# Two stages of a hybrid block stack read their 256-token operands from addresses 64 bytes off a multiple of 128

## The chip, the cores and the metric

One NeuronCore of a Trainium2 chip runs the whole program in a single launch. The metric is the device time of one execution in microseconds. The kernel before takes 2101.51 us, the median of three runs (2100.49 to 2103.12). One execution was profiled; all rows below come from it.

## The reference, cut to what matters

The program computes two layers of a hybrid block (chunk attention, a depthwise convolution and a retention mixer, then a squared-ReLU MLP) and one layer of a second block (differential attention beside a state-space layer, then a gated feed-forward with a 3-tap convolution) on 512 tokens of width 1024, all in float32. The two stages that the change is about are these:

```python
# first block, second of two layers, after the mixers
x = x + rms_norm(mix, g_mix_post)
h = rms_norm(x, g_mlp_pre)                                  # (512, 1024)
f = jnp.square(jax.nn.relu(h @ w_up)) @ w_down              # w_up 1024 x 4096, w_down 4096 x 1024
# second block
hn = rmsnorm(h, norm2_gain[i])
up = causal_dwconv(hn @ w_up[i], conv_w[i], conv_b[i])      # w_up 1024 x 5632
gate, val = jnp.split(up, 2, axis=-1)
h = h + (jax.nn.silu(gate) * val) @ w_down[i]               # w_down 2816 x 1024
```

## The kernel before, in words

**Precision.** Every float32 operand is split in two float32r parts, a rounded one (names ending in `hi`) and the rest (`lo`), and a product is three matmuls: weights hi by input hi, weights hi by input lo, weights lo by input hi (`mm3`). A matmul holds a 128 x 128 operand in the array and streams a moving operand of N columns, one column per token or per output feature. A row such as `ps<-hhi,whi` reads: into PSUM tile `ps`, moving operand `hhi`, held operand `whi`.

**The transposed input.** After each norm, `to_hT` transposes the normed tokens and writes them to `hhi` and `hlo`, two tiles of 128 partitions x 8 x 512 (features by tokens) that live for the whole program. The projections of the mixers use them as moving operand with all 512 tokens, as held operand (for outputs that keep tokens on the partitions, the weights then stream in 384 or 512 columns), and at a stage's start by halves of 256 tokens.

**The two fast stages.** The MLP of the second hybrid layer and the feed-forward of the second block compute `h @ w_up` by a Strassen-like scheme with seven products in place of eight (`FastUp`): a unit makes two output tiles of 128 features x 512 tokens from seven products of 256 tokens each, four of them with halves of `hhi` and `hlo`, three with sums of blocks. `fast_in` makes the sums once a stage: `shi` and `slo`, twelve tiles of 128 x 512. The first four output tiles of each stage are computed plainly, in halves of 256 tokens (`f_split`). So every up-projection matmul of these stages streams 256 columns. The down-projections between them stream weights in 512 columns, with `fhi` and `flo` held.

**What sets the order.** The Python code does not issue instructions; `Trace` records them with a due time. `order` then plans: it walks through time with its own costs, gives a free engine the ready instruction that is due first, chooses between ScalarE, VectorE and GpSimd where an instruction may run on more than one of them, and gives each tile a slot of its pool at its first instruction. An instruction whose tile finds no free slot, or whose slot an earlier one is promised, is passed over (`room`). The planned list is issued as it stands (line 674 is the one line that issues, so all rows of the profile carry it); each engine runs its own part of the list in order.

**Where tiles lie.** Pools are laid out one after the other. Tiles of the pool without slots (`cp`) lie where they are first placed; `mhalf`, `hhi` and `hlo` are placed first. Behind them come the weight pools and `sp`, 58 general slots of 2048 bytes per partition for nearly every other tile (`s2` takes from it), then small ones. `hhi` starts at byte 2304 of a partition, `hlo` at 18688, the slots of `sp` from 104192 on: all multiples of 128. Slices of them start at multiples of 512 bytes. So each float32r moving operand of the program starts at a multiple of 128 bytes.

Of the kernel before, what the change touches and what calls it, by code (L numbers as in the profile page):

```python
# [11 lines left out]
F32R = mybir.dt.float32r  # L12
# [5 lines left out]
P = 128  # L18
S = 512
# [917 lines left out]
class Builder:  # L937
# [11 lines left out]
    def __init__(self, tc, ctx, A, out):  # L949
        self.tc, self.nc, self.A, self.out = tc, Trace(tc.nc), A, out  # L950

        def pool(name, bufs, shape=None, dtype=F32, space="SB"):
            kw = {} if space == "SB" else {"space": bass.MemoryType.PSUM if space == "PS" else bass.MemoryType.DRAM}
            return Pool(lambda n: ctx.enter_context(tc.tile_pool(name=n, bufs=1, **kw)), name, bufs, shape, dtype, space)
        self.cp = pool("cp", None)
        self.wr = pool("wr", self.NR, [P, 1024])
        self.wh, self.wl = pool("wh", self.NW, [P, 1024], F32R), pool("wl", self.NW, [P, 1024], F32R)
        self.sp = pool("sp", 86 - 2 * self.NR - 4 * self.NW, [P, 512])
        self.stp = pool("stp", 16, [P, 32])
        self.jp = pool("jp", 2, [P, 512], BF16)  # L960
        self.psp = pool("psp", 4, [P, 512], F32, "PS")
        self.pss = pool("pss", 4, [P, 512], F32, "PS")
        self.dp = pool("dp", None, space="DRAM")
        self.side = Side(self)
        self.T = 30000.0
        self.in_side = False
        self.wbias = 2
        self.rawT = None
        self.before = None
        self.seven = False  # L970
# [164 lines left out]
    def fast_in(self):  # L1135

        nc, R = self.nc, self.rawT
        self.rawT = None
        S = {}
        for j in range(2):  # L1140
            s1, s2, s4, s3 = (self.s2(name="sraw") for _ in range(4))
            nc.sub(s1, R[1, j], R[1, j + 2], self.wbias)
            nc.sub(s2, s1, R[0, j], self.wbias)
            nc.sum(s4, R[0, j + 2], s2, self.wbias)
            nc.sub(s3, R[0, j], R[1, j], self.wbias)
            for i, s in ((6, s2), (5, s1), (3, s4)):
                hi, lo = self.s2(F32R, "shi"), self.s2(F32R, "slo")
                nc.copy(hi, s)
                nc.sub(lo, s, hi.bitcast(F32), self.wbias)
                S[i, j] = [z.rearrange("p (k n) -> p k n", k=2) for z in (hi, lo)]  # L1150
            hi, lo = (z[:, 2 * j:2 * j + 2, 256:512] for z in (self.hhi, self.hlo))
            v = s3.rearrange("p (k n) -> p k n", k=2)
            nc.copy(hi, v)
            nc.sub(lo, v, hi.bitcast(F32), self.wbias)

        def a(i, k):
            if i == 1:
                return self.hT(k, 0, 256)
            if i == 2:
                return self.hT(k + 4, 0, 256)  # L1160
            if i == 4:
                return self.hT(k + 4, 256, 512)
            if i == 7:
                return self.hT(k, 256, 512)
            return tuple(z[:, k % 2, :] for z in S[i, k // 2])
        return a
# [11 lines left out]
    def fast_end(self, steps=(4, 3)):  # L1178
        if self.before:
            for i in steps:  # L1180
                self.before.run(i)
            if 3 in steps:
                self.before = None

    def run(self):
        nc, tc, A = self.nc, self.tc, self.A
        self.pvt = self.cp.tile(F32, "pv", [P, PV_N])
        self.cm = self.cp.tile(F32, "cm", [P, 4 * P])
        self.rope = self.cp.tile(F32, "rope", [P, NT, 64])
        self.hhi = self.cp.tile(F32R, "hhi", [P, KD, S])  # L1190
        self.hlo = self.cp.tile(F32R, "hlo", [P, KD, S])
        self.mhalf = self.cp.tile(F32, "mhalf", [P, 32])
        self.ident = self.cm[:, 0:P]
        self.blk64 = self.cp.tile(F32R, "blk64", [P, P])
        self.blk16 = self.cm[:, 2 * P:3 * P]
        self.tri = self.cm[:, 3 * P:4 * P]
        self.ones = self.cp.tile(F32R, "ones", [P, P])
        self.epsc = self.cp.tile(F32, "epsc", [P, 1])
        self.ws = Stream(self, A["wst"], stream_spec())
        X = [[self.s2(name="X") for _ in range(2)] for _ in range(NT)]  # L1200
        gpre = [self.s2(name="gain") for _ in range(2)]

        def load_x(t):
            for h in range(2):
                nc.sync.dma_start(out=X[t][h], in_=A["x"][t * P:(t + 1) * P, 512 * h:512 * (h + 1)])
        nc.vector.memset(self.mhalf, -0.5)
        nc.vector.memset(self.ones.bitcast(F32), 1.0)
        nc.vector.memset(self.epsc, EPS)
        self.prio(-8000.0)
        load_x(0)  # L1210
        for h in range(2):
            nc.sync.dma_start(out=gpre[h], in_=A["gains"][0, :, 512 * h:512 * (h + 1)])
        nc.sync.dma_start(out=self.ident, in_=A["cmat"][:, 0:P])
        self.prio(0.0)
        load_x(1)
        hs = {}
        for t in range(2):
            hs[t] = self.pre_norm(t, X, gpre)
            self.to_hT(t, hs.pop(t))
        self.prio(4000.0)  # L1220
        self.wbias = 3
        self.ws.prep_to(2)
        self.prio(8000.0)
        for t in (2, 3):
            load_x(t)
            hs[t] = self.pre_norm(t, X, gpre)
        self.prio(20000.0)
        nc.sync.dma_start(out=self.pvt, in_=A["pvec"])
        nc.sync.dma_start(out=self.cm[:, P:], in_=A["cmat"][:, P:])
        nc.vector.tensor_copy(self.blk64, self.cm[:, P:2 * P])  # L1230
        nc.sync.dma_start(out=self.rope, in_=A["rope2"].rearrange("t p n -> p t n"))
        del X
        self.pending = hs
        self.xd = None
        self.prio(self.T)
        for l in range(LAYERS):
            self.hybrid(l)
        self.second()
# [294 lines left out]
    def hybrid(self, l):  # L1533
# [8 lines left out]
            return tt  # L1542
        tabs = []
        for t in range(NT):
            z = self.s2(name="rtab")
            nc.sync.dma_start(out=z[:, :RT_N], in_=A["rtab"][t])
            tabs.append(z)

# [24 lines left out]

        def rot(w):
            def f(t, ps):
                d = self.s2(name="rqk")
                self.ret_rot(t, ps, w, tabs[t], d)
                qk[w].append(d)
            return f
# [39 lines left out]
        self.t_unit(lambda t, ps: p0.__setitem__(t, ps), 512, mix, 4, W_OUT_KS, need)  # L1619
        self.side.drain()  # L1620
        self.rawT = {} if l in FAST else None
        self.finish(lambda t: (p0[t],), 4, W_OUT_KS, mix, X, gpost, gpre)
        self.mix = {}
        (self.mlp if l in FAST else self.mlp_plain)(l, X)
# [152 lines left out]

    def finish_mlp(self, f, acc, xm, gpost, gpre, store):
        nc = self.nc
        ks = sorted(f)  # L1780
        lhs = lambda k, t0, t1: tuple(z[:, t0:t1] for z in f[k])
        nch = len(ks) // 2
        ws = [self.ws.take() for _ in range(2 * nch)]
        hs, X = {}, {}
        for t in range(NT):
            X[t] = [self.s2(name="X") for _ in range(2)]
            for h in range(2):
                nc.sync.dma_start(out=X[t][h], in_=xm[t][h])
                ps = self.ps()
                for c in range(nch):  # L1790
                    self.t_part(ps, ws[h * nch + c], ks[2 * c:2 * c + 2], t, 512, lhs, c == 0, c == nch - 1)
                nc.vector.tensor_tensor(acc[t][h], ps, acc[t][h], op=ALU.add)
            self.post_update(t, acc[t], X, gpost)
            if 1 <= t <= 2:
                self.to_hT(t - 1, hs.pop(t - 1))
            hs[t] = self.pre_norm(t, X, gpre)
            store(t, X)
            X.pop(t)
        self.pending = hs
# [246 lines left out]
    def dq_evac(self, p, t, ps, cg, sg):  # L2046
# [5 lines left out]
        nc.vector.tensor_scalar(st[:, 0:8], st[:, 0:8], EPS, None, op0=ALU.add)  # L2052
        nc.gpsimd.tensor_tensor(st[:, 8:16], st[:, 0:8], self.mhalf[:, :8], op=ALU.pow)
        nc.vector.tensor_scalar(self.rq[:, p, :, t], st[:, 8:12], 0.125, None, op0=ALU.mult)
        a, b, d = self.s2(), self.s2(), self.s2(name="dqk")
        v4 = lambda z: z.rearrange("p (a g d) -> p a g d", a=2, d=64)
        tb = lambda z: z.rearrange("p (a d) -> p a d", a=2).unsqueeze(2).to_broadcast([P, 2, 4, 64])
        nc.vector.tensor_tensor(v4(a), v4(ps), tb(cg[:, t * P:(t + 1) * P]), op=ALU.mult)
# [71 lines left out]
    def second(self):  # L2130
# [11 lines left out]
        self.nlam = st[:, 5:6]  # L2142
        nc.vector.tensor_scalar(st[:, 6:7], self.pvt[:, PV["subln"][0]:PV["subln"][0] + 1], 1.0 - LAM_INIT, None, op0=ALU.mult)
        self.subl = st[:, 6:7]
        self.mask = self.s2(name="mask")
        nc.gpsimd.memset(self.mask[:, :384], 0.0)
        nc.gpsimd.tensor_copy(self.mask[:, 384:], self.tri)
        self.rq = self.cp.tile(F32, "rq", [P, 4, 4, NT])
        cg, sg = self.s2(name="cg"), self.s2(name="sg")
        go = PV["gqk"][0]  # L2150
        gv = self.pvt[:, go:go + 128].rearrange("p (a d) -> p a d", d=32)
        for t in range(NT):
# [116 lines left out]
        ws = [self.ws.take() for _ in range(4)]  # L2269
        hs = {}  # L2270
        self.rawT = {}
        for t in range(NT):
            ps = self.ps()
            for c in range(4):
# [54 lines left out]
@with_exitstack  # L2329
def hybrid_stack_kernel(ctx: ExitStack, tc, A, out):  # L2330
    b = Builder(tc, ctx, A, out)
    b.run()
    order = b.nc.order()
    for t in (b.mhalf, b.hhi, b.hlo):
        t.place()
    with tc.manual_schedule():
        b.nc.issue(order)
# [18 lines left out]
```

## Time and profile before

| | |
|---|---|
| runs | 2100.49, 2101.51, 2103.12 us; median 2101.51 |
| the profiled execution | 2105.0 us, its span from the first to the last instruction 2103.3 us |
| TensorE (PE) | busy 2015.8 us, 96% of the span, 11188 matmuls; mean granted clock 0.988 of 2.4 GHz |
| weight loads (PEld) | 1745.7 us, beside the matmuls |
| VectorE (DVE) | 1527.6 us, 73% |
| ScalarE (ACT) | 1042.0 us, 50% |
| GpSimd (POOL) | 691.8 us, 33% |
| fast stage of the first block | up to 1215 us; its matmuls of 256 columns begin at about 890 us |
| fast stage of the second block | from about 1740 us to the end |

Matmuls overlap: the duration of one holds the way through the array too, so a stream of matmuls is read by the distance from one start to the next, and busy time says only that PE never stood still.

### The profile page before, as it was taken

How to read it: one execution, taken by the hardware profiler on the slowest of the kernel's cores; microseconds unless marked ns; L12 is line 12 of the kernel's file. 1: busy time of each engine (PE TensorE's matmuls, PEld its weight loads, DVE VectorE, ACT ScalarE, POOL GpSimd, SP SyncE). 2: the span in 40 equal slices, each digit the busy share in tenths (PEclk: the TensorE clock that was granted, in tenths of full speed). 3: DMA queues.
4: the chain of work that ended last, by engine and by line, in shares of the span. 5: the costliest groups of instructions: out<-in, count | busy, mean ns of one | idle time of the engine just before them, and what ended most of it. 6: DMA issues, size and time to landing. Idle time of an engine off the chain costs nothing. (4 is left out here: it accounts for less than half of the span.)

```text
span 2103.3 us, 29992 instructions
## 1 busy us (share of the span) xinstructions
PE 2015.8 (96%) x11188; PEld 1745.7 (83%) x11188; DVE 1527.6 (73%) x2485; ACT 1042.0 (50%) x1773; POOL 691.8 (33%) x846
## 2 busy tenths in 40 slices
PE   7999889999999999999999999999999999999999
PEld 7987788778888987799988987677777889989998
DVE  5999695344457999576776773678688649889887
ACT  3378434222233388564444444366477326545543
POOL 4662357960014662200000037763753430000000
PEclk9999989999999999999999999999999999999999
DMA  5423334333242423332423564232425521333322
GB/s 191 133 61 120 122 105 129 112 110 100 80 126 91 133 62 121 98 91 81 132 89 101 180 197 125 71 96 60 120 65 156 163 87 61 101 101 101 121 79 92
DMA packets 87873, 229.53 MB, mean 109 GB/s; under 512 B 10672, under 2 KB 20656, under 8 KB 87728
## 3 DMA queue, kind: packets, MB, share of 16 engines
q1 hardware_dynamic: 87728, 227.62, 34.4%
q8 instruction: 88, 1.44, 0.3%
q14 instruction: 57, 0.47, 0.1%
HBM read 206.35 MB, written 21.23 MB: 108 GB/s over the span
## 5 line engine op out<-in xcount | busy, mean ns | idle before, releaser
L674 ACT CAST whi<-wraw 128x1024 fp32r<-128x1024 f32 (+1 forms) x324 | 332.0, 1031 | 448.2 <-PE ps L674 373.6
L674 POOL TENSOR_TENSOR wlo<-wraw,whi 128x1024 fp32r<-128x1024 f32 (+1 forms) x144 | 337.1, 2347 | 526.3 <-ACT whi L674 433.6
L674 PE MATMUL ps<-hhi,whi 128*128 128x256 f32 (+1 forms) x1488 | 454.9, 331 | 7.2 <-ACT hhi L674 2.3
L674 PE MATMUL ps<-hlo,whi 128*128 128x256 f32 (+1 forms) x1488 | 452.3, 329 | 9.6 <-DVE hlo L674 9.6
L674 PE MATMUL ps<-hhi,wlo 128*128 128x256 f32 (+1 forms) x1488 | 449.8, 328 | 1.2 <-DVE wlo L674 1.2
L674 PEld LDWEIGHTS ps<-hlo,whi 128*128 128x128 f32 x1488 | 273.1, 194 | 34.1 <-DVE hlo L674 10.9
L674 PEld LDWEIGHTS ps<-hhi,whi 128*128 128x128 f32 x1488 | 273.4, 194 | 33.5 <-ACT hhi L674 3.3
L674 PEld LDWEIGHTS ps<-hhi,wlo 128*128 128x128 f32 x1488 | 271.9, 193 | 24.2 <-DVE wlo L674 1.4
L674 DVE TENSOR_TENSOR wlo<-wraw,whi 128x1024 fp32r<-128x1024 f32 x190 | 235.8, 1247 | 59.7 <-ACT whi L674 59.5
L674 PE MATMUL ps<-whi,fhi 128*128 128x512 f32 x688 | 251.0, 392 | 7.5 <-DVE t L674 4.4
L674 PE MATMUL ps<-wlo,fhi 128*128 128x512 f32 x688 | 251.9, 392 | 1.6 <-DVE wlo L674 1.6
L674 PE MATMUL ps<-whi,flo 128*128 128x512 f32 x688 | 252.4, 392 | 0.0
L674 DVE TENSOR_TENSOR acc<-ps,acc 128x512 f32<-128x512 f32 x112 | 76.1, 687 | 122.9 <-PE ps L674 122.8
L674 PE MATMUL ps<-whi,hhi 128*128 128x384 f32 (+1 forms) x448 | 154.5, 370 | 5.2 <-DVE vlo L674 3.5
L674 PE MATMUL ps<-wlo,hhi 128*128 128x384 f32 (+1 forms) x448 | 154.9, 369 | 1.2 <-POOL wlo L674 1.2
L674 PEld LDWEIGHTS ps<-whi,fhi 128*128 128x128 f32 x688 | 129.1, 188 | 31.4 <-DVE t L674 4.8
L674 PE MATMUL ps<-whi,hlo 128*128 128x384 f32 (+1 forms) x448 | 153.7, 369 | 0.0
L674 PEld LDWEIGHTS ps<-wlo,fhi 128*128 128x128 f32 x688 | 129.8, 189 | 26.6 <-DVE wlo L674 2.9
L674 PEld LDWEIGHTS ps<-whi,flo 128*128 128x128 f32 x688 | 129.7, 189 | 24.3
L674 PE MATMUL ps<-shi,whi 128*128 128x256 f32 (+1 forms) x440 | 124.3, 292 | 0.6 <-ACT mid L674 0.6
L674 PE MATMUL ps<-slo,whi 128*128 128x256 f32 (+1 forms) x440 | 124.2, 291 | 0.0
L674 PE MATMUL ps<-shi,wlo 128*128 128x256 f32 (+1 forms) x440 | 124.0, 290 | 0.0
(272 smaller groups left out, 3896.8 us busy)
## 6 DMA issues: line engine op xcount, KB each, us to landing
wraw<-in_wst SPq DMA_DIRECT2D x302, 512.0 KB, 3.7
wraw<-in_wst SPq DMA_DIRECT2D x32, 384.0 KB, 3.1
gain<-in_gains SPq DMA_DIRECT2D x20, 256.0 KB, 4.7
X<-in_x SPq DMA_DIRECT2D x16, 256.0 KB, 5.2
xd<-X SPq DMA_DIRECT2D x16, 256.0 KB, 2.4
X<-xd SPq DMA_DIRECT2D x16, 256.0 KB, 6.1
gated<-t SPq DMA_DIRECT2D x16, 256.0 KB, 3.0
gate<-gated SPq DMA_DIRECT2D x16, 256.0 KB, 4.2
```

The source lines that it names most:

```text
L674: getattr(getattr(self.nc, e), m)(*[r(x) for x in op.args], **{k: r(v) for k, v in op.kw.items()})
```

## The change

The edits are three. First, `hhi` and `hlo` become tiles that are 32 elements longer, and `shift(n)` chooses the view that starts n elements in: n = 16 (64 bytes) before the transposes that feed the two fast stages, n = 0 everywhere else. Second, the slots of `sp` fall from 58 to 46, and a new pool `sq` of 12 slots is laid out last, behind a pad of 16 elements, so that its slots start at byte 202816 and on, 64 past a multiple of 128. `shi` and `slo` take their slots there; in the other stages the rotation tables (`rtab`), the rotated queries and keys (`rqk`, `dqk`), the mask and two small tables (`cg`, `sg`) do. Third, `hlo` moves from byte 18688 to 18816, still a multiple of 128 where it isn't shifted.

```diff
-        self.sp = pool("sp", 86 - 2 * self.NR - 4 * self.NW, [P, 512])
+        self.sp = pool("sp", 74 - 2 * self.NR - 4 * self.NW, [P, 512])
         self.stp = pool("stp", 16, [P, 32])
         self.jp = pool("jp", 2, [P, 512], BF16)
+        self.pad = pool("pad", 1, [P, 16])
+        self.sq = pool("sq", 12, [P, 512])
...
-                hi, lo = self.s2(F32R, "shi"), self.s2(F32R, "slo")
+                hi, lo = self.sq.tile(F32R, "shi"), self.sq.tile(F32R, "slo")
...
+    def shift(self, n):
+
+        self.hhi, self.hlo = (z[:, n:n + KD * S].rearrange("p (k n) -> p k n", k=KD) for z in self.hbig)
+
...
-        self.hhi = self.cp.tile(F32R, "hhi", [P, KD, S])
-        self.hlo = self.cp.tile(F32R, "hlo", [P, KD, S])
+        self.hbig = [self.cp.tile(F32R, n, [P, KD * S + 32]) for n in ("hhi", "hlo")]
+        self.shift(0)
...
+        nc.vector.memset(self.pad.tile(name="pad"), 0.0)
...
-            z = self.s2(name="rtab")
+            z = self.sq.tile(name="rtab")
...
-                d = self.s2(name="rqk")
+                d = self.sq.tile(name="rqk")
...
         self.rawT = {} if l in FAST else None
+        self.shift(16 if l in FAST else 0)
         self.finish(lambda t: (p0[t],), 4, W_OUT_KS, mix, X, gpost, gpre)
...
     def finish_mlp(self, f, acc, xm, gpost, gpre, store):
         nc = self.nc
+        self.shift(0)
...
-        a, b, d = self.s2(), self.s2(), self.s2(name="dqk")
+        a, b, d = self.s2(), self.s2(), self.sq.tile(name="dqk")
...
-        self.mask = self.s2(name="mask")
+        self.mask = self.sq.tile(name="mask")
...
-        cg, sg = self.s2(name="cg"), self.s2(name="sg")
+        cg, sg = self.sq.tile(name="cg"), self.sq.tile(name="sg")
...
         self.rawT = {}
+        self.shift(16)
...
-    for t in (b.mhalf, b.hhi, b.hlo):
+    for t in [b.mhalf] + b.hbig:
         t.place()
```

Since the planner now finds 46 general slots and 12 reserved ones, it makes another order in three places: the mixers of the two hybrid layers (in the trace of before, 122 to 225 us and 751 to 854 us) and part of the attention and state-space stage of the second block (1283 to 1630 us). Everywhere else, in both fast stages too, PE's list is the same instruction by instruction. PE has as many instructions as before; ACT loads its function tables 45 times in place of 43.

In the first of the three places, this is VectorE's list while the retention heads and the end of the convolution branch run (`cacc`, `csq`, `crs` belong to the convolution's layer norm, `ptlo` and `rysq` to a retention pair, `vhl` to the attention's values):

```order
 L674 TENSOR_TENSOR xlo<-ctot,xhi 128x512
-L674 TENSOR_TENSOR ptlo<-ps,pthi 128x512
+L674 TENSOR_TENSOR xlo<-rysq,xhi 128x512
+L674 TENSOR_TENSOR vhl<-ps,vhl 128x4x64
+L674 SCALAR_TENSOR_TENSOR cacc<-ps,cacc 128x512 x2
+L674 TENSOR_TENSOR vhl<-ps,vhl 128x2x64
+L674 TENSOR_TENSOR xlo<-csq,xhi 128x512
+L674 RECIPROCAL crs<-crs 128x512
+L674 RECIPROCAL rysq<-rysq 128x512
```

The convolution's norm, its long reciprocal with it, now stands ahead of the later retention splits, which it followed before.

ScalarE's list at the same place (`pthi` are retention scores, `crs` the convolution's square root, `cacc` its activation):

```order
+L674 CAST xhi<-csq 128x512
+L674 ACT_TABLE_LOAD
+L674 ACTIVATE crs<-ps,epsc 128x512
+L674 CAST whi<-wraw 128x1024
+L674 ACTIVATE rysq<-ps,epsc 128x512
+L674 CAST pthi<-ps 128x512
+L674 CAST vhl<-ps 128x4x64
 L674 CAST pthi<-ps 128x384
+L674 CAST whi<-wraw 128x1024 x2
+L674 ACT_TABLE_LOAD
+L674 ACTIVATE cacc<-cacc,pv 128x512 x2
```

The same norm moved ahead here, and the table loads for its square root and activation moved with it.

## Rows read from the trace of the kernel before

**Rows 1.** The page: span, and busy time of each engine
```profile
span 2103.3 us, 29992 instructions
...
PE 2015.8 (96%) x11188; PEld 1745.7 (83%) x11188; DVE 1527.6 (73%) x2485; ACT 1042.0 (50%) x1773; POOL 691.8 (33%) x846
```

**Rows 2.** Stretches: length, then each engine's busy us (instructions), clock, DMA share, GB/s
```profile
122.00:225.00 103.00, 96.52 (x492) 80.05 (x492) 94.92 (x179) 79.23 (x151) 40.22 (x46) 1.00 0.29 95
751.00:854.00 103.00, 97.60 (x497) 80.39 (x496) 92.45 (x181) 80.19 (x152) 40.97 (x49) 1.00 0.30 97
1283.00:1630.00 347.00, 327.47 (x1538) 252.90 (x1537) 258.41 (x483) 211.68 (x379) 198.97 (x153) 0.99 0.31 93
905.00:1205.00 300.00, 299.99 (x1922) 273.18 (x1922) 211.83 (x306) 145.34 (x222) 0.68 (x2) 1.00 0.36 112
1750.00:2078.00 328.00, 322.95 (x2270) 300.86 (x2269) 291.52 (x424) 184.20 (x286) 0.00 (x0) 1.00 0.29 95
```

**Rows 3.** Starts of matmuls of 256 columns, about 1850 us: start, duration us, instruction
```profile
1850.65 0.28 PE L674 MATMUL ps<-shi,whi 128*128 128x256 f32 x1
...
1851.85 0.28 PE L674 MATMUL ps<-slo,whi 128*128 128x256 f32 x1
```

**Rows 4.** Starts of matmuls of 512 columns, about 520 us
```profile
519.69 0.39 PE L674 MATMUL ps<-hhi,whi 128*128 128x512 f32 x1
...
521.96 0.39 PE L674 MATMUL ps<-whi,flo 128*128 128x512 f32 x1
```

**Rows 5.** Starts of matmuls of 384 columns, about 60 us
```profile
59.69 0.33 PE L674 MATMUL ps<-whi,hlo 128*128 128x384 f32 x1
...
61.43 0.33 PE L674 MATMUL ps<-whi,hhi 128*128 128x384 f32 x1
```

**Rows 6.** Groups of matmuls, 880 to 1215 us: count | busy us, mean ns
```profile
L674 PE MATMUL ps<-hhi,wlo 128*128 128x256 f32 x288 | 75.2, 286 | 0.0
...
L674 PE MATMUL ps<-slo,whi 128*128 128x256 f32 x168 | 44.4, 283 | 0.0
```

**Rows 7.** The same groups, 1740 to 2090 us
```profile
L674 PE MATMUL ps<-hhi,whi 128*128 128x256 f32 x384 | 99.8, 285 | 1.7 <-ACT mid L674 1.1 <-ACT cu L674 0.6
...
L674 PE MATMUL ps<-shi,whi 128*128 128x256 f32 x240 | 68.4, 285 | 0.6 <-ACT mid L674 0.6
```

**Rows 8.** Starts of 256-column matmuls at two other moments of the second stage
```profile
1859.50 0.29 PE L674 MATMUL ps<-shi,whi 128*128 128x256 f32 x1
1859.63 0.28 PE L674 MATMUL ps<-slo,whi 128*128 128x256 f32 x1
1859.74 0.28 PE L674 MATMUL ps<-shi,wlo 128*128 128x256 f32 x1
...
1864.41 0.27 PE L674 MATMUL ps<-hhi,whi 128*128 128x256 f32 x1
1864.52 0.28 PE L674 MATMUL ps<-hlo,whi 128*128 128x256 f32 x1
```

**Rows 9.** Tile `shi`, 905 to 1205 us: durations in ns, min/median/max
```profile
L674 PE MATMUL ps<-shi,whi x168: 277/283/287, 920.1 to 1192.3; 128*128 128x256 f32 x168
...
L674 PE MATMUL ps<-shi,wlo x168: 274/283/287, 920.3 to 1192.6; 128*128 128x256 f32 x168
```

**Rows 10.** PE's longest wait in 122 to 225, 1283 to 1630, 1750 to 2078: us, times, longest
```profile
PE ps L674 <- DVE row L674: 3.9, 4, 1.6
...
PE ps L674 <- DVE row L674: 10.1, 7, 5.1
...
PE ps L674 <- DVE wlo L674: 2.8, 4, 1.2
```

**Rows 11.** Groups of ACT's table loads and of a small VectorE memset: count | busy us, mean ns
```profile
L674 ACT ACT_TABLE_LOAD x43 | 55.2, 1283 | 7.4 <-DVE st L674 5.1 <-PE ps L674 0.9 <-PEq L2348 0.8
...
L674 DVE MEMSET epsc<- 128x1 f32 x1 | 0.1, 59 | 0.0
```

## The prediction

> **What bounds the kernel now.** I read the busy times of the page first [rows 1]: PE is busy 96% of the span, no other engine over 73%. The next view is busy time by stretch [rows 2]. In the first fast stage PE is busy 299.99 of 300 us, in the second 322.95 of 328, with the clock granted in full (1.00, the 2.4 GHz level). There the time is the number of matmuls times the distance from one start to the next, and nothing else. In the three stretches whose order changes PE is idle for 6.5, 5.4 and 19.5 us, and in the first two VectorE is busy 94.9 and 92.5 of 103 us, so there PE and VectorE share the bound.
>
> The third view is the list of starts. Ten matmuls of 256 columns lie in 1.20 us, 120 ns each [rows 3]; ten of 512 columns in 2.27 us, 227 ns [rows 4]; ten of 384 columns in 1.74 us, 174 ns [rows 5]. From 256 to 512 columns the distance grows by 107 ns, 0.417 ns a column, which is one column a cycle at 2.4 GHz. What is left is the same at every width: 120 − 106.7 = 13.3 ns, 227 − 213.3 = 13.7, 174 − 160 = 14. So each matmul pays a toll of some 13.3 ns, as much as 32 columns, or 128 bytes of the float32r operand, and a 256-column matmul pays 11% of its time for it. A stage agrees: 905 to 1205 us has 1922 matmuls, of which about 1281 have 256 columns and 641 have 512; 1281 x 120 + 641 x 227 = 299.2 us.
>
> The toll isn't quite fixed. Close by, two starts lie 130 and 110 ns behind the one before [rows 8], which at the view's 10 ns step only says that it moves; the first 256-column matmul after a change of width has 110 ns to the next. The durations say it more finely: median 283, lowest 274, highest 287 ns [rows 9], at a length that else is the distance plus some 163 ns. So distances of about 111 to 124 ns do happen with the same operand width and tile.
>
> The Trainium skill, page "TensorE: Matmul & The Clock Gate", section "Back-to-back issue gap", gives a warm matmul N/2.4 + 2.5 ns. This trace differs: it has 13.3 ns where the page has 2.5. If the shift brought the page's toll, the first term below would be 10.8 ns x 3240 = 35 us instead of 21.6, an estimate from that page.
>
> **The change part by part.**
>
> *The rate of 256-column matmuls.* Those whose moving operand comes to lie 64 bytes off: in the first stage three groups of 288 with `hhi` or `hlo` and three of 168 with `shi` or `slo` [rows 6], 1368; in the second three of 384 and three of 240 [rows 7], 1872; together 3240. What the start address does to the toll no row shows, since every moving operand of that kind starts at a multiple of 128 bytes now. The bounds are the extremes of the durations against their median [rows 9]: −9 ns and +4 ns each, so −29.2 and +13.0 us. I choose a toll that falls by half, 64 of its 128 bytes, 16 columns or 6.7 ns: it is a toll at the start of a stream, its size is a whole stretch of 128 bytes, and distances of 110 ns to 120 ns are what the streams fall to when something else has upset their phase. 3240 x 6.67 = −21.6 us. All of it lies on the path, since PE never stands still there, but for the next term.
>
> *What is late next.* In the second stage VectorE is busy 291.5 of 328 us. With 1872 x 6.67 = 12.5 us less, it would be busy 291.5 of 315.5, 92%. PE's largest wait there is for `wlo`, the low weight parts that VectorE makes: 2.8 us in 4 waits [rows 10]. I add 2 us; the ends are 0 and 5 us (the idle of that stretch once more). In the first stage VectorE is busy 211.8 us, of 291 then: 73%, nothing added.
>
> *The three reordered stretches.* PE waits there for `row` (scores on VectorE) most: 3.9 us in the first, 10.1 in the third [rows 10]. The convolution's norm, with a reciprocal and its table loads, moves ahead of retention splits on VectorE and ScalarE, and two table loads of 1.28 us are added [rows 11]; ScalarE is busy 79 of 103 us, so it can take them, but what queues behind them on ScalarE (score casts, weight casts) and on VectorE goes to PE. The work of a stretch is the same, so the order can win at most the idle of 31.4 us, and cost about as much; a third of it either way, ±10 us, is what I keep as ends. I take +2, the loads' price once.
>
> *At nothing.* The pad's memset: one as small takes 59 ns [rows 11], at the start where VectorE waits for loads. The 112 transposes that hold `rqk` or `dqk` from a shifted slot: 112 x 6.7 ns is under 1 us either way, in stretches where PE waits anyhow. Some 290 instructions of VectorE, ScalarE and GpSimd touch a shifted tile; they are hidden behind PE, and if each cost 16 elements more, some 20 ns, the sum on all three engines would be 6 us, of which the full stretches could pass on 2. The shifted views overlap the unshifted ones, so a write into the new place may wait for reads of the old one; all those reads belong to projections that end before the norms start, so no wait is added.
>
> Sum: −21.6 + 2 + 2 = −17.6 us. Against the profiled execution, 2105.0 us with 1.7 us around its span, that is 2087; that execution lies 3.5 us over the median of the runs, so against 2101.5 it is 2084.
>
> **The rivals.**
>
> *A quarter.* Durations and starts fall in steps of 3 to 4 ns (274, 277, 283, 287). If the shift moves the stream by one step, 3.3 ns, the gain is 10.8 us; with the other terms 2095. For it: 277 is a step that both groups of rows 9 show. Against: it leaves most of the toll.
>
> *The whole toll.* If every one runs as the fastest one does, −29.2 + 5 for a VectorE that is then busy 94%: 2077. For it: the 274 ns row. Against: it happens rarely, and after a change of width only. The page on TensorE named above has a toll smaller still.
>
> *No change of rate.* The toll may be that of changing the held operand, which every one of these matmuls does, and then the address of the moving one is nothing to it. For it: 13.3 to 14 ns at all widths, on all tiles. What is left is the reordering, +2 on 2101.5: 2104, from 2094 to 2112. The Trainium skill, page "SBUF — State Buffer", section "Door 1: The DMA port swizzle", speaks for this one: it has SBUF read in lines of 16 bytes, and a shift by 64 is four whole lines, so nothing would change. The trace can't tell, having no such operand.
>
> *Slower.* An operand of 1024 bytes that starts 64 off a grid of 128 touches nine pieces where it touched eight. If the toll comes from pieces of that size, each matmul pays 4 to 6.7 ns more (the highest duration, or half a piece): 13 to 21.6 us on 3240, on PE's path in full, since no other engine bounds it. 2115 to 2125, say 2119. It decides as soon as the median of these durations lies above 283 ns.
>
> **How the numbers follow.** Forecast, half the toll, 2084: 0.42. A quarter, 2095: 0.18. The whole, 2077: 0.08. No change of rate, 2104: 0.20. Slower, 2119: 0.12. A measurement of this kernel tells some 0.2% from no change, 4.2 us: faster means under 2097.3, slower over 2105.7. Faster: 0.42 + 0.08 + two thirds of 0.18, 0.62. No change: the rest of the quarter and half of "no change of rate", 0.16. Slower: 0.22. The forecast's own range is 2076 to 2094. For eight in ten it reaches to 2068, which takes in the fastest case with a lucky order, and to 2112, the upper end of "no change of rate"; "slower" is left out.
>
> **What would show it.** Right: in both fast stages 256-column matmuls start 113 ns apart in the list of starts, their median duration is some 276 ns, those of 512 columns stay at 389 and 227 ns, the stretch of 1922 matmuls takes 291 us instead of 300, and PE's waits for `wlo` in the last stage rise by some 2 us. Wrong: the same 120 ns with the toll elsewhere, a median above 283, or a gain given back in waits for `wlo` and `row`. The 256-column matmuls at the start of the unfast stages (`hhi` unshifted) must stay at 120 ns in the same trace; if they fall too, the address isn't the cause.

## The result: 3% slower, and the loss is in the mixers

The changed kernel takes 2164.12 us (median of 4 runs, 2162.41 to 2171.20), the kernel before 2101.60 beside it (4 runs). The ratio is 1.0300, 95% interval 1.0283 to 1.0317. The prediction said 2084, with 2068 to 2112 as its range: wrong in sign, and 52 us beyond the range.

The page of the kernel after: the span, and the busy time of each engine.

```profile
span 2169.1 us, 30101 instructions
...
PE 2049.4 (94%) x11188; PEld 1766.5 (81%) x11188; DVE 1534.6 (71%) x2493; ACT 1040.1 (48%) x1769; POOL 691.2 (32%) x845
```

VectorE, ScalarE and GpSimd do the work of before to within 7 us [rows 1]. PE has the same 11188 matmuls and is busy 33.6 us longer, and the span is 65.8 us longer. So half of the loss is PE standing still, and half is PE being busy longer with the same matmuls. The profiled execution of the kernel after is the slowest of its four, 7 us over their median, so its spans add up to a few us more than the loss of 62.5 us by the medians.

The stretches of the kernel after that begin at the same matmuls as those of [rows 2], in the same columns: length, busy us (instructions) of PE, PEld, DVE, ACT and POOL, granted clock, DMA share, GB/s. In order: the mixers of the two layers, the attention stretch of the second block, and 300 and 328 us of the two fast stages.

```profile
121.00:255.00 134.00, 110.72 (x495) 88.96 (x494) 94.30 (x178) 78.76 (x149) 43.05 (x47) 0.87 0.23 74
780.00:917.00 137.00, 113.15 (x497) 90.61 (x496) 100.47 (x181) 77.22 (x147) 42.73 (x49) 0.86 0.24 73
1346.70:1696.60 349.90, 331.39 (x1538) 257.47 (x1537) 255.51 (x481) 209.82 (x376) 199.28 (x152) 0.96 0.30 89
...
968.00:1268.00 300.00, 299.59 (x1930) 272.50 (x1930) 212.40 (x308) 145.39 (x223) 0.81 (x2) 1.00 0.36 115
1819.50:2147.50 328.00, 322.34 (x2287) 300.16 (x2287) 294.33 (x429) 184.85 (x287) 0.00 (x0) 1.00 0.29 95
```

The first mixer does in 134 us what took 103. PE is idle for 23.3 us of it (134 − 110.72) where it was 6.5, and busy 110.72 us where it was 96.52, for 495 instructions and 492: 16.8 us more idle time and 14.2 us more busy time make the 31. The second mixer has 18.5 and 15.5 us. The third stretch differs: with the same 1538 matmuls PE is idle for 18.5 us where it was 19.5, and its 3 us more come with a clock of 0.96 where it was 0.99. In the fast stages, where the whole gain was expected, little has changed: 300 us of the first hold 1930 matmuls where they held 1922, and in the second PE is idle for 5.7 us of 328 where it was 5.1.

Why PE is busy longer stands in the clock column, taken in pieces of 20 us of the first mixer after the change (same columns; the last line is a shorter piece inside the third):

```profile
121.00:141.00 20.00, 18.71 (x84) 14.87 (x82) 14.44 (x13) 10.99 (x16) 13.27 (x11) 1.00 0.39 123
141.00:161.00 20.00, 12.79 (x54) 9.98 (x54) 11.09 (x17) 12.57 (x20) 5.71 (x14) 0.83 0.08 26
161.00:181.00 20.00, 14.69 (x57) 11.95 (x58) 14.47 (x19) 11.27 (x20) 7.34 (x17) 0.74 0.17 54
181.00:201.00 20.00, 15.97 (x77) 12.44 (x75) 14.71 (x31) 11.72 (x25) 7.18 (x3) 0.99 0.40 119
201.00:221.00 20.00, 17.48 (x76) 14.41 (x77) 12.79 (x32) 8.72 (x22) 0.16 (x1) 0.75 0.11 39
221.00:241.00 20.00, 18.02 (x77) 14.50 (x76) 14.53 (x39) 13.56 (x24) 4.62 (x2) 0.83 0.32 106
...
163.20:173.00 9.80, 6.08 (x20) 5.22 (x21) 7.59 (x10) 3.82 (x7) 5.14 (x17) 0.50 0.19 54
```

In 161 to 181 us the clock granted is 0.74 on average: 0.50, the lower level of 1.2 GHz, from 163.2 to 173, and 2.4 GHz else; in the slice ahead of it PE had been idle for 7.2 of 20 us. By the list of starts, the distances between matmuls without a gap add up to 11.2 us more than in the kernel before, and all of that lies in the parts at 1.2 GHz, 34 us together. Most of the other 3 us are the ends of matmuls that no next one covers: PE stops 18 times where it stopped 7 times. In the second mixer the two shares are 12.8 and 2.8 us. No engine is full in the worst slices: VectorE, which bounded this stretch with PE before, is busy 11 to 14.5 of 20 us. So nothing is overloaded; work that used to lie side by side now lies one behind the other.

The list of starts shows it (start, duration in us, instruction, in brackets the idle time before it and what ended it). First PE of the kernel after around 160 us; `khi,stk` are a retention head's scores, `hhi`, `hlo` the projections:

```profile
159.67 0.40 PE L674 MATMUL ps<-hlo,whi 128*128 128x512 f32 x1
159.90 0.39 PE L674 MATMUL ps<-hhi,wlo 128*128 128x512 f32 x1
162.04 0.44 PE L674 MATMUL ps<-khi,stk 128*128 128x384 f32 x1 [1.75 <-ACT rysq L674]
162.32 0.33 PE L674 MATMUL ps<-klo,stk 128*128 128x384 f32 x1
166.04 0.58 PE L674 MATMUL ps<-khi,stk 128*128 128x256 f32 x1 [3.39 <-DVE ptlo L674]
166.42 0.42 PE L674 MATMUL ps<-klo,stk 128*128 128x256 f32 x1
166.64 0.41 PE L674 MATMUL ps<-khi,stk 128*128 128x256 f32 x1
166.85 0.41 PE L674 MATMUL ps<-klo,stk 128*128 128x256 f32 x1
167.06 0.52 PE L674 MATMUL ps<-khi,stk 128*128 128x384 f32 x1
```

Then VectorE at the same moment:

```profile
160.10 0.69 DVE L674 CAST whi<-wraw 128x1024 fp32r<-128x1024 f32 x1 [1.55 <-PE ps L674]
162.09 3.35 DVE L674 RECIPROCAL rysq<-rysq 128x512 f32<-128x512 f32 x1 [1.29 <-ACT rysq L674]
165.36 1.09 DVE L674 TENSOR_TENSOR ptlo<-ps,pthi 128x512 fp32r<-128x512 f32 x2
```

PE makes two score matmuls and then waits until VectorE has done the 3.35 us reciprocal and the split `ptlo` behind it. The next scores of 256 columns start 210 to 220 ns apart (166.42, 166.64, 166.85), and 256 columns at 1.2 GHz are 213 ns: they run at the lower clock. In the kernel before, projections lay between such scores. Counting only matmuls with the tile `hhi` (first column pair: PE), the same 20 us of the kernel before and of the kernel after:

```profile
162.00:182.00 20.00, 13.52 (x43) 7.66 (x42) 0.00 (x0) 0.00 (x0) 1.00 0.63 225
```

```profile
161.00:181.00 20.00, 5.31 (x16) 3.00 (x16) 0.00 (x0) 0.00 (x0) 0.74 0.17 54
```

43 matmuls to fill in then, 16 now. The projections aren't fewer in the stretch; more of them stand at its start (49 in the first 20 us, 32 before) and in 201 to 241 us (32, where in 202 to 222 us before there were none). PE's waits of the kernel after (total us, times, longest), first in 121 to 255 us, then in 780 to 917 us, are what PE loses by it:

```profile
PE o L674 <- DVE ptlo L674: 8.4, 4, 6.1
PE ps L674 <- DVE row L674: 7.3, 3, 5.3
PE ps L674 <- DVE ptlo L674: 3.7, 2, 3.4
...
PE ps L674 <- DVE row L674: 7.3, 3, 5.3
PE o L674 <- DVE ptlo L674: 5.6, 4, 3.4
PE ps L674 <- DVE xlo L674: 5.1, 2, 4.6
```

The longest wait for `row` was 1.6 us in the first mixer before [rows 10]; now it is 5.3, and one for `ptlo` 6.1, where the longest was 1.4.

The rate, on which the prediction rested, moved little. Two starts ten matmuls apart in the kernel after, in the stretch of [rows 3]:

```profile
1851.20 0.28 PE L674 MATMUL ps<-shi,wlo 128*128 128x256 f32 x1
...
1852.38 0.28 PE L674 MATMUL ps<-hhi,wlo 128*128 128x256 f32 x1
```

and the durations of tile `shi` in its first fast stage (min/median/max in ns), which answer to [rows 9]:

```profile
L674 PE MATMUL ps<-shi,whi x168: 276/279/283, 982.7 to 1253.3; 128*128 128x256 f32 x168
L674 PE MATMUL ps<-shi,wlo x168: 276/280/286, 982.9 to 1253.6; 128*128 128x256 f32 x168
```

That is 118 ns where 120 stood, and a median 3 to 4 ns lower; the forecast was 113 ns and 276.

### The profile page after: what moved, and what is told of

The parts are those of the page before. It is cut to its first block, busy times and chain, and to the rows that moved or that the text cites. A ratio compares the mean times of both kernels' runs of the same rounds, so it can differ in the third digit from the quotient of the medians.

```text
span 2169.1 us, 30101 instructions
## 1 busy us (share of the span) xinstructions
PE 2049.4 (94%) x11188; PEld 1766.5 (81%) x11188; DVE 1534.6 (71%) x2493; ACT 1040.1 (48%) x1769; POOL 691.2 (32%) x845
## 5 line engine op out<-in xcount | busy, mean ns | idle before, releaser
L674 ACT CAST whi<-wraw 128x1024 fp32r<-128x1024 f32 (+1 forms) x317 | 324.5, 1030 | 436.5 <-PE ps L674 365.6
L674 POOL TENSOR_TENSOR wlo<-wraw,whi 128x1024 fp32r<-128x1024 f32 (+1 forms) x143 | 332.7, 2333 | 593.5 <-ACT whi L674 479.2
L674 PEld LDWEIGHTS ps<-whi,fhi 128*128 128x128 f32 x688 | 129.2, 188 | 31.4 <-DVE t L674 4.8
```

What stands on the lines that cost most here:

```text
L674: getattr(getattr(self.nc, e), m)(*[r(x) for x in op.args], **{k: r(v) for k, v in op.kw.items()})
```

## The experiments

One table holds what all runs gave. The stretches are times between the same places (numbers of matmuls) in PE's list in the one profiled execution of each kernel, in us; where an order still differs at such a place (e4, e5, e8, e11, e12), that moves a mixer by up to 3 us. The distances are means in ns over the list of starts, of matmuls that began without a gap (some 3840 of 256 columns that stream `hhi`, `hlo`, `shi` or `slo`, 870 of 384, 4880 of 512). The ratio is to the kernel before on the same chip.

| kernel | time, us | ratio, 95% interval | mixers | second block | fast stages | 256 / 384 / 512 columns |
|---|---|---|---|---|---|---|
| before | 2101.60 | 1 | 102.7, 102.5 | 328.9 | 323.6, 332.0 | 119.5 / 174.2 / 228.4 |
| after | 2164.12 | 1.0300 [1.0283, 1.0317] | 133.3, 136.7 | 333.4 | 321.6, 328.3 | 117.8 / 175.8 / 229.2 |
| e1 shift, old slots | 2100.92 | 0.9991 [0.9983, 1.0000] | 102.6, 102.7 | 328.8 | 321.3, 329.9 | 118.2 / 175.8 / 229.3 |
| e2 new slots, no offset | 2165.12 | 1.0297 [1.0283, 1.0311] | 134.4, 136.8 | 328.9 | 321.3, 329.7 | 118.2 / 175.8 / 229.3 |
| e3 offsets, old order | 2104.70 | 1.0009 [0.9999, 1.0018] | 102.8, 102.8 | 329.8 | 321.1, 328.6 | 117.8 / 175.8 / 230.4 |
| e4 50 slots | 2179.41 | 1.0364 [1.0350, 1.0378] | 134.7, 141.3 | 328.9 | 323.7, 331.8 | |
| e5 54 slots | 2147.18 | 1.0208 [1.0191, 1.0225] | 122.2, 128.5 | 330.5 | 323.3, 331.8 | |
| e6 59 slots | 2099.58 | 0.9979 [0.9968, 0.9989] | 102.2, 99.8 | 328.9 | 323.7, 331.8 | |
| e7 rows in reserved | 2142.91 | 1.0179 [1.0157, 1.0201] | 121.1, 122.8 | 335.1 | 321.0, 328.4 | |
| e8 values in reserved | 2115.21 | 1.0059 [1.0041, 1.0078] | 112.6, 110.9 | 329.2 | 321.0, 328.4 | |
| e9 base moved | 2103.25 | 1.0000 [0.9992, 1.0009] | 102.7, 102.7 | 330.0 | 322.1, 330.3 | 118.4 / 175.7 / 229.3 |
| e10 later pools moved | 2103.82 | 1.0004 [0.9995, 1.0013] | 102.6, 102.6 | 327.9 | 323.6, 332.1 | 119.5 / 174.3 / 228.3 |
| e11 both in reserved | 2097.51 | 0.9970 [0.9958, 0.9982] | 100.0, 101.2 | 332.8 | 321.6, 328.3 | 117.7 / 175.8 / 229.4 |
| e12 as e11, no offset | 2098.13 | 0.9979 [0.9968, 0.9990] | 100.0, 101.1 | 332.8 | 321.5, 329.7 | 118.2 / 175.8 / 229.3 |

**e1, the shifted input alone.** The general slots and the order are those of before.

```diff
-        self.hhi = self.cp.tile(F32R, "hhi", [P, KD, S])
-        self.hlo = self.cp.tile(F32R, "hlo", [P, KD, S])
+        self.hbig = [self.cp.tile(F32R, n, [P, KD * S + 32]) for n in ("hhi", "hlo")]
...
+        self.shift(16 if l in FAST else 0)
...
```

> Only the transposed input is shifted by 64 bytes in the two fast stages; pools, slots and every engine's order are those of before, and the block sums stay at multiples of 128. Slots theory (the loss is the split of the slots, the address helps a little): 2016 of the 256-column matmuls gain some 2 ns each, so 2097.4 us, 0.2% faster than before; their starts 118 ns apart, those of the block sums 120. Address theory (a shifted operand costs somewhere, in its writes or in the reordered stages): slower than before, up to 2165. Chance theory (any change of the planner's input reshuffles the list): nothing to reshuffle here, 2097 as well.

Measured: 0.9991, at the edge of what can be told, where 0.2% was expected. The 256-column distances fall as expected, to 118.2 ns, but e9 below has 118.4 without the shift, and those of 384 and 512 columns rise. The mixers stay at 102.6 and 102.7 us: the loss isn't in this part of the change.

**e2, the new pools and their order, with all operands at multiples of 128 bytes.**

```diff
-        self.pad = pool("pad", 1, [P, 16])
+        self.pad = pool("pad", 1, [P, 32])
...
-        self.shift(16 if l in FAST else 0)
+        self.shift(0)
...
```

> The 46 general and 12 reserved slots and the order of the changed kernel, with every operand back at a multiple of 128 bytes. Slots theory: 2164 + 6.7 = 2171 us, all 256-column starts 120 ns apart, the two mixer stretches as long as in the changed kernel (133 and 137 us). Address theory: back near 2101 to 2110, the mixer stretches 103 us.

Measured: 2165.12 us, mixers at 134.4 and 136.8. The whole loss is there without one operand at an odd multiple of 64: it comes from the slots and the order made from them. What I expected the missing offset to cost isn't there: the run lies 1 us from the kernel after.

**e3, the offsets in the order of before.** The plan is made with 58 shared slots; afterwards the tiles are given other slots, so that the block sums get 12 that lie 64 bytes off.

```diff
...
+    recolor(b.sp, order, b.nc.ops)
...
```

> All 3240 operands of the changed kernel lie 64 bytes off a multiple of 128, but 58 slots stay shared: the plan and every engine's order are those of before, and only afterwards each tile is given a slot so that the block sums get one of 12 shifted slots and other tiles the rest or those 12 when they are free. Slots theory: 3240 x 2.06 ns = 6.7 us gained and nothing lost, 2095 us, faster than before by 0.3%. Address theory: 2150 or more, since the shifted operands are all there. Chance theory: 2095 too.

Measured: 1.0009, no change, where 2095 was expected. The mixers stay at 102.8 us, and no gain comes from the addresses: the 256-column matmuls are as fast as in the kernel after, but those of 512 columns take 230.4 ns, where before has 228.4 and e1, with the same order, 229.3. Part of that is some 350 matmuls whose held operand came to lie 64 bytes off, at 233.1 ns; the others take 230.1.

**e4, fewer slots and nothing else.**

```diff
-        self.sp = pool("sp", 86 - 2 * self.NR - 4 * self.NW, [P, 512])
+        self.sp = pool("sp", 78 - 2 * self.NR - 4 * self.NW, [P, 512])
```

> The kernel before with 50 shared slots instead of 58, nothing else. Slots theory: the mixer stretches hold up to 58 live tiles in before, so fewer retention and attention chains run side by side; slower, 2115 to 2150, less than the changed kernel, with PE waiting for ptlo and row in the mixer stretches. Chance theory: a reshuffle like any other, anywhere in 2095 to 2170. Address theory: no operand moves off its multiple of 128, so 2101.

Measured: 2179.41 us, more than expected, and in the same two places. Taking slots away makes the loss without an operand off its multiple of 128 and without the new pool. The first mixer in the run with 50 slots:

```profile
122.00:257.00 135.00, 110.36 (x491) 88.46 (x490) 99.24 (x178) 79.85 (x151) 43.42 (x50) 0.87 0.24 74
```

The same picture as in the kernel after: PE busy 110.4 of 135 us at a clock of 0.87.

A rival was left: that any newly made order would lose as much, the one of before being a lucky one. The next five runs put it against the slots.

**e5, 54 slots** (the same line with 82).

> The kernel before with 54 general buffers of 2 KB in place of 58, nothing else edited; the scheduler makes another order from it. Slots theory (the mixers lose because too few general buffers stand free for the next chain of work, so the loss grows with the buffers taken away): between the kernel before (58, 2102 us) and the run with 50 (2179 us), so 2115 to 2160 us, each mixer stretch at 107 to 130 us where 58 buffers have 102.6 and 50 have 135 to 141. Chance theory (the order of before is a lucky one, and any newly made order loses about as much whatever the count): 2150 to 2185 us, mixers at 130 to 141 us as with 50.

**e6, 59 slots** (the same line with 87).

> The kernel before with 59 general buffers in place of 58; the scheduler makes another order from it. Slots theory: one more buffer cannot hurt, 2092 to 2103 us, mixer stretches at 100 to 103 us. Chance theory: a new order is again an unlucky one, 2140 to 2185 us with mixers at 120 to 140 us.

Measured: 2147.18 and 2099.58 us. The first mixers, with 54 slots and with 59:

```profile
122.00:244.00 122.00, 106.24 (x488) 84.69 (x488) 96.45 (x174) 79.88 (x152) 43.80 (x48) 0.94 0.27 83
```

```profile
121.00:223.00 102.00, 95.96 (x490) 79.73 (x490) 93.83 (x175) 79.88 (x153) 40.77 (x46) 1.00 0.30 96
```

The two mixers together take 276.0, 250.7, 205.2 and 202.0 us with 50, 54, 58 and 59 slots. The clock rises with them, 0.87, 0.94, 1.00, 1.00. An order that was made anew with 59 isn't slow. The chance theory falls, which gave 2150 to 2185 us for the first and 2140 to 2185 for the second.

**e7, the attention's row tiles in reserved slots,** in the changed kernel.

```diff
-        rows = self.rows(self.s2(name="row")[:, :256])
+        rows = self.rows(self.sq.tile(name="row")[:, :256], self.sq)
...
```

> The changed kernel, in which the attention's row tiles (a pair for each third of a head group, of tag row) also take reserved buffers, so that some of the 12 that stand idle late in each mixer are used and the 46 general ones are relieved. Slots theory: part of the 63 us comes back, 2115 to 2155 us, mixers at 108 to 132 us. Chance theory: another new order, as slow as the others, 2155 to 2185 us.

**e8, the attention's packed values in reserved slots.**

```diff
-            V.append(self.v_pack(ps))
+            V.append(self.v_pack(ps, self.sq))
...
```

> The changed kernel, in which the packed values of the attention (tag vhl) take reserved buffers instead of general ones: they live through the whole attention of a mixer, so they relieve the 46 for longest, once the block sums have left the 12. Slots theory: part of the 63 us comes back, 2110 to 2150 us, mixers at 106 to 130 us; if the packs must wait for the block sums to leave their buffers, the loss moves there and the time stays at 2160 us or over. Chance theory: 2155 to 2185 us.

**e11, both.**

> The changed kernel, in which the packed values of the attention and its row tiles take reserved buffers (the two edits that were run apart, 2115 and 2143 us). Slots theory: more of the idle 12 are used, 2095 to 2115 us, each mixer stretch at 101 to 111 us; where the 12 become too few for both, 2115 to 2135 us. Chance theory (a new order is slow for no reason of buffers): 2130 to 2185 us.

Measured: 2142.91, 2115.21, and 2097.51 us with both, all three times within what the slots theory gave. The mixers of e11:

```profile
122.00:222.00 100.00, 97.67 (x491) 80.02 (x490) 91.80 (x175) 81.27 (x154) 43.73 (x48) 1.00 0.34 104
748.00:849.00 101.00, 98.39 (x494) 80.26 (x493) 90.55 (x178) 81.82 (x154) 44.33 (x50) 1.00 0.32 101
```

PE is idle for 2.3 and 2.6 us in them, less than in the kernel before, and the clock is granted in full. There are 46 general slots and 12 reserved ones as in the changed kernel; only what may use the 12 differs. A count, from the planned lists, of the slots that hold a tile says why: in the kernel before, up to all 58 are in use in a mixer; in the changed kernel the general ones stand at 40 to 46 of 46 for most of the first mixer, while the 12 hold 8 tiles at its start and none from the 800th matmul on (the mixer is matmuls 673 to 1162). In e11 they hold mostly 8 to 12 nearly to its end. This version is 0.3% faster than the kernel before, with an interval that ends below 1; its interval and that of e6 overlap.

**e9, the longer input tiles without the shift.** `hlo` begins 128 bytes later and the pools behind it 256; no operand lies at an odd multiple of 64. Against e1:

```diff
-        self.shift(16 if l in FAST else 0)
+        self.shift(0)
...
```

> The run with only the transposed input shifted, without the shift: both tiles of it are 128 bytes longer as there, so the low half begins 128 bytes later and every pool behind it 256 bytes later, but no matmul operand lies at an odd multiple of 64. The order of before. Address theory (the odd multiples of 64 raise the rate): the 256-column matmuls go back to 119.5 ns, the first and second fast stage to 323.6 and 332.0 us, time 2102 to 2104 us, same as before. Base theory (the rate follows where the pools lie modulo 512 bytes, and the 64 are worth 1 ns a matmul or less): 118.2 to 118.9 ns, the 512-column ones at 229.3 ns, fast stages 321 to 322 and 329.5 to 330.5 us, time 2100 to 2102 us.

**e10, the later pools moved alone.** Both halves of the input stay where they were.

```diff
+        self.hbig = [self.cp.tile(F32R, n, [P, KD * S + e]) for n, e in (("hhi", 0), ("hlo", 64))]
...
```

> The kernel before with 256 bytes left free behind the low half of the transposed input, so that both halves of it stay where they are and only the pools behind them move by 256 bytes, from 256 to 0 modulo 512. The order of before. Base theory: the 256-column matmuls take 118.2 to 118.9 ns (119.5 before), the 512-column ones 229.3 (228.3), the 384-column ones 176.4 (174.1), as in the runs with the moved pools. If the move of the low half by 128 bytes did it: 119.5, 228.3 and 174.1 ns, all as before, and 2102 to 2104 us.

Measured: e9 has distances of 118.4, 175.7 and 229.3 ns, e10 119.5, 174.3 and 228.3, as before. The two have the same order and differ in where `hlo` lies. So the rates moved with `hlo`, from byte 18688 to 18816, and not with the later pools as I had thought: 1.1 ns less for 256 columns, 1.4 and 1.0 ns more for 384 and 512. Of the loss at 512 columns, 4.7 us in all, 2.7 lie in the 532 matmuls that stream `hlo` itself (228.1 ns before, 233.1 in e9). 300 us of the first fast stage that begin at the same matmul as the fourth line of [rows 2], in e9 and in e10:

```profile
907.00:1207.00 300.00, 299.86 (x1929) 272.98 (x1929) 212.92 (x308) 145.31 (x223) 0.69 (x2) 1.00 0.36 114
```

```profile
904.70:1204.70 300.00, 299.99 (x1922) 273.16 (x1921) 211.83 (x306) 145.28 (x222) 0.68 (x2) 1.00 0.36 112
```

They hold 1929 and 1922 matmuls; the kernel before has 1922. Neither time can be told from that of the kernel before (1.0000 and 1.0004).

**e12, e11 without the offsets,** in the order of e11. Against e11:

```diff
-        self.pad = pool("pad", 1, [P, 16])
+        self.pad = pool("pad", 1, [P, 32])
...
-        self.shift(16 if l in FAST else 0)
+        self.shift(0)
...
-        self.shift(16)
+        self.shift(0)
```

> The run with the packed values and the row tiles in reserved buffers (2097.5 us), in the same order, with every matmul operand at a multiple of 128 bytes: the transposed input is not shifted, and the pad ahead of the reserved buffers is 128 bytes in place of 64. It prices the odd multiples of 64 apart from the order. By the prediction's address theory the 3240 matmuls of 256 columns would lose 6.67 ns each again: 2117 to 2119 us. By the rates measured in the two runs of the changed pools (117.6 to 118.2 with the offset, 118.4 to 118.7 ns without), they lose about 0.8 ns each, 2 to 3 us: 2098 to 2101 us, second fast stage at 329.7 us for 328.3.

Measured: 2098.13 us, by the rates and not by the prediction's address theory. The odd multiples of 64 are worth 0.44 ns a matmul of 256 columns (118.18 to 117.74, and 118.22 to 117.78 between e2 and the kernel after), some 1.7 us on 3840, and the two times can't be told apart. That is a mean of unlike parts: from e12 to e11 the distance to the next start falls by 1.8 ns behind matmuls that stream `hlo` and by 1.2 behind those with `shi`, and rises by 0.6 behind those with `hhi`.

## Why the prediction was wrong

*The step that failed: "The three reordered stretches".* It took +2 us, within ±10, and the stretches measured +30.7, +34.1 and +4.5 us in the profiled executions, 69 in all. It reasoned that the work is the same, "so the order can win at most the idle of 31.4 us, and cost about as much". The first half is a bound; the second isn't. A gain is limited by the idle time that is there, but a loss by how much overlap there is to undo, and in a mixer PE and VectorE were busy 96.5 and 94.9 of 103 us side by side. The step then priced what it saw in the order, two table loads, and didn't ask why the planner had made another order: 12 of 58 slots were taken out of a store that had none to spare, and given to tiles that don't need them in a mixer's second half. Runs e4 to e6 show that the number of slots alone does this, and e7, e8 and e11 that giving the 12 back undoes it. The table loads weren't the price: e11 has 47, four more than the kernel before, and the lowest time of all runs.

```profile
L674 ACT ACT_TABLE_LOAD x47 | 60.3, 1283 | 6.5 <-DVE st L674 4.9 <-PEq L2358 0.8
```

The 4.5 us of the third stretch aren't the order's: e2 has the order of the kernel after and 328.9 us there, as before.

*The price of idle time.* The step had no term for the clock. In the mixers PE was busy 14.2 and 15.5 us longer, near half of the loss, and 11.2 and 12.8 of that is the lower clock, granted at 0.74 to 0.83 on average in the slices in or behind which PE had idled. Each microsecond that PE waited in a mixer cost nearly two.

*The rate.* The term of −21.6 us is mis-sized, and its cause is mostly another. It rested on a toll that falls by half when the start moves by 64 bytes; no row showed that, and the runs don't. The kernel after gains 1.74 ns a matmul of 256 columns, 6.7 us on 3846, but loses 0.88 ns on 4855 of 512 columns (4.3 us) and 1.5 ns on 851 of 384 (1.3 us): −1.1 us. Only 0.44 of the 1.74 ns are the offset's; 1.1 come with `hlo` moved by 128 bytes, in e9, without any offset, and the last 0.2 (118.4 in e9, 118.2 in e2, with the new pools and their order) weren't taken apart. The fast stages, where most of the 256-column matmuls are, won 2.0 and 3.7 us. The rival "No change of rate" was closest for this term. "Slower" had the sign of the result, but by luck: its cause was an address toll of 13 to 21.6 us, which no run shows, and 2164 lies 39 us over its upper end. The prediction's own test caught it: the unshifted 256-column matmuls fell as well, from 119.4 to 118.3 ns (`hhi`), so the shift isn't the main cause. Nor is what a matmul takes beyond one column a cycle the same at every width, as the prediction read it from ten starts each: by the means it is 12.8, 14.2 and 15.1 ns at 256, 384 and 512 columns before, and 11.1, 15.8 and 15.9 after. Two slips of the working matter little: the whole-toll rival leaves out the +2 for the order (2079, not 2077), and the rows shown have 277 ns as the lowest duration of one group only.

*What held.* The bound of the fast stages is PE, at the distances read from the starts; VectorE didn't become the bound in the second (PE's waits for `wlo` there are 3.2 us, 2.8 before). The shifted views added no wait, and the memset and the transposes from shifted slots cost nothing that shows. The mean effect of the offset has the sign that was forecast, at a fifteenth of the size (0.44 ns for 6.67).

*What stays open.* Why the place of `hlo` changes the rate of matmuls that don't read it: `shi` matmuls went from 119.5 to 118.9 ns in e9. Why the third stretch had a lower clock in the one profiled execution of the kernel after. Why 50 shared slots (276 us for the mixers) are worse than 46 with 12 reserved (270 us), was not tried apart.

## What to carry to other kernels

When slots are set aside for one kind of tile, count how many of the shared ones are in use at the fullest moment and what the reserved ones hold then: a scheduler that runs short of buffers loses overlap, and the loss isn't bounded by the idle time that was there (here 6.5 us in a mixer that lost 31). When a diff changes a planned order, ask what constraint made the planner change it, before pricing the instructions that moved. A reservation is cheap if tiles that live long at the moments of shortage may use it too: here that turned 1.030 into 0.997 of the time.

## What the runs showed of the hardware

- The mean start-to-start distance of this program's float32r matmuls moves a little with where operands lie, at multiples of 128 bytes too: with `hlo` at byte 18816 in place of 18688 (e9), 256 columns take 118.4 ns for 119.5, 384 take 175.7 for 174.2, and 512 take 229.3 for 228.4.
- Moving operands at odd multiples of 64 bytes gain 0.44 ns a matmul of 256 columns on average (e12 to e11), with both signs among the tiles. Matmuls of 512 columns with a held operand at an odd multiple have 233.1 ns, the others of the same run 230.1 (e3, some 350 and 4500); but the 532 that stream `hlo` have 233.1 in e9 too, where nothing lies at an odd multiple.
- No placement that was tried took more than 1.8 ns off what a 256-column matmul takes beyond one column a cycle at 2.4 GHz: 119.5 − 106.7 = 12.8 ns before, 11.0 at best (e11).
- PE's granted clock fell to 1.2 GHz four times in the first mixer after the change, 34 us together, with PE idle for 23.3 of 134 us; with 6.5 of 103 us idle before, it stayed at 1.00.
